# The feed-forward blocks of a two-layer encoder in two sweeps, with the gate and value products in a seven-product form

## The chip, the cores and the metric

One Trainium2 chip, one core. The metric is device microseconds (us) of one execution of the whole program. Several executions of the kernel before were timed, and one was recorded by the hardware profiler; all rows below are of that one.

## What is computed

Two layers over the same 1024 prompt tokens and 64 sample tokens. Each layer is a mixer (layer 0: retention and differential attention; layer 1: band attention and a state-space scan), a product with an output matrix, and a feed-forward block. Only the feed-forward block changes:

```python
x = x + g1 * mixer_out                              # 1024 features
h = rmsnorm(x, norm_g[l, 1]) * (1.0 + sc2) + sh2    # scale and shift from the modulation w_mod[l]
u = h @ w_up[l]                                     # 1024 -> 2 * 2816
a, g = u[..., :2816], u[..., 2816:]
g = causal_dwconv(g, past, conv_w, conv_b)          # width 3, along the tokens
x = x + g2 * ((a * gelu(g)) @ w_down[l])            # 2816 -> 1024
```

All is fp32. A product is emulated by splitting each operand into a high and a low fp32r part and adding three matmuls (high by high, low by high, high by low).

## The kernel before, in words

Activations lie feature-major: 128 features a tile, tokens along the columns, in three chunks c of 386, 386 and 324 columns (two columns of overlap for the convolution, the sample tokens at the end of chunk 2). `x` stays in SBUF for the whole feed-forward block.

The output product (`out_proj`, PSUM tile `ops`) adds into `x` chunk by chunk, and `norm_chunk` follows each chunk: squares on ACT, sums (`nacc`) on POOL and DVE, a transposing matmul `nps`, the reciprocal root on DVE and POOL, a broadcast matmul `nbc`, then `nt` on DVE and the split into `hhi` and `hlo`.

The block itself (`ffn`) goes over 11 pairs j of two 128-column tiles of `w_up`. For each pair it makes the gate tiles (`gps`, six groups of 24 matmuls), the down product of the pair before it (`dps`, 24 groups of 6 matmuls of up to 384 columns, each added into `x` by DVE), and the value tiles (`aps`, six groups of 24). The gated product `yhi`, `ylo` stays in SBUF for one pair; the last two pairs go down together. So a pair is 288 matmuls up and 144 down, and the down product always lies between gate and value products. While chunk 2 is still being normalized, pair 0 works on chunks 0 and 1.

A weight tile (`raw`, 1 MB) is loaded on SP's queue, cast to `whi` on ACT, and its `wlo` is subtracted on POOL, one instruction of 128x2048.

In layer 0 the modulation of layer 1 runs beside the block: 24 units, each two loads `mh`, 16 multiply-adds `macc` of 128x256 on DVE, and a few small matmuls; `side` is called after every group and takes a step at every fourth.

The engines run their instructions in order; the order is set by the scheduler from the written program.

Of the kernel before, what the change touches and what calls it, by code (L numbers as in the profile page):

```python
# [17 lines left out]
P = 128  # L18
# [21 lines left out]
NWA = 10  # L40
NST = 6
# [4 lines left out]
FS = 4  # L46
# [18 lines left out]
NW = 23  # L65
# [43 lines left out]
class PsPools:  # L109
# [7 lines left out]
    def tile(self, tag, name):  # L117
        if tag == "g":
            turn = self.turns[self.n % len(self.turns)]
            self.n += 1  # L120
            if turn:
                return self.shared.tile([P, 512], F32, tag="gs", name=name)
        p, shape = self.t[tag]
        return p.tile(shape, F32, tag=tag, name=name)


def build(ctx, tc, A, O, stop=None):
# [309 lines left out]
    def x_load(xp):  # L437
        x = [xp.tile([P, KT, CN[c]], F32, tag=f"x{c}", name=f"x{c}") for c in range(3)]
        for c in (2, 0, 1):
            for ks in (slice(4, 8), slice(0, 4)):  # L440
# [3 lines left out]
    def resid(x, c, m, ps, gate):  # L444
        for (b, e, s) in SEG[c]:
            stt(x[c][:, m, b:e], ps[:, b:e], gate[:, m, s:s + 1], x[c][:, m, b:e], ALU.mult, ALU.add)

    def out_proj(w, a, x, gate, pp, after, wts):
        def unit(u, c):
            for m in range(2):  # L450
                ps = pp.tile("g", "ops")
                gemm_fm(ps, wts[u], P * m, a[c], CN[c])
                resid(x, c, 2 * u + m, ps, gate)
# [9 lines left out]
    def ffn(l, a, x, gate, pp, w, after, side):  # L463
        ys = {}
        step = [0]

        def tick():
            side(step[0], pp)
            step[0] += 1

        def down(js):
            wds = [load_rows(A["w_down"][l], 256 * j) for j in js]
            for c in range(3):
                n = CN[c]
                for m in range(KT):
                    ps = pp.tile("g", "dps")
                    mms = []
                    for j, (whi, wlo) in zip(js, wds):
                        for k in range(2):
                            yhi, ylo = ys[j, c, k]  # L480
                            wh, wl = whi[:, k, P * m:P * m + P], wlo[:, k, P * m:P * m + P]
                            mms += [(wh, yhi), (wh, ylo), (wl, yhi)]
                    for i, (lt, rh) in enumerate(mms):
                        T.matmul(out=ps[:, 2:n], lhsT=lt, rhs=rh[:, 2:n], start=(i == 0), stop=(i == len(mms) - 1))  # L484
                    resid(x, c, m, ps, gate)
                    tick()
                if js[-1] == NPAIR - 1:
                    after(c)
            for j in js:
                for c in range(3):  # L490
                    for k in range(2):
                        ys.pop((j, c, k))

        ge = {}

        def up_gate(j, wg, c):
            n = CN[c]
            for m in range(2):
                f = 2 * j + m
                ps = pp.tile("g", "gps")  # L500
                gemm_fm(ps, wg, P * m, a[c], n, b=0)
                e = ge[c, m] = w("ge")
                S.activation(out=e[:, :n], in_=ps[:, :n], func=AF.Identity, scale=fcw[l][:, 2, f:f + 1], bias=fcb[l][:, f:f + 1])  # L503
                stt(e[:, 1:n], ps[:, 0:n - 1], fcw[l][:, 1, f:f + 1], e[:, 1:n], ALU.mult, ALU.add)
                stt(e[:, 2:n], ps[:, 0:n - 2], fcw[l][:, 0, f:f + 1], e[:, 2:n], ALU.mult, ALU.add)
                if c == 2:
                    V.tensor_add(e[:, 260:262], e[:, 260:262], fcor[l][:, f, :])
                    tail = ps[:, 256:388].rearrange("p (s x) -> p s x", x=66)[:, :, 0:2]
                    V.tensor_copy(fo[l][:, :, :, f], tail)
                S.activation(out=e[:, :n], in_=e[:, :n], func=AF.Gelu_apprx_tanh)  # L510
                tick()

        def value(j, wa, c):
            n = CN[c]
            for m in range(2):
                ps = pp.tile("g", "aps")
                gemm_fm(ps, wa, P * m, a[c], n)
                e = ge.pop((c, m))
                hi, lo = w("yhi", F32R), w("ylo", F32R)
                V.tensor_mul(e[:, 2:n], ps[:, 2:n], e[:, 2:n])  # L520
                S.copy(hi[:, 2:n], e[:, 2:n])  # L521
                G.tensor_tensor(out=lo[:, 2:n], in0=e[:, 2:n], in1=hi[:, 2:n].bitcast(F32), op=ALU.subtract)  # L522
                ys[j, c, m] = (hi, lo)
                tick()

        for j in range(NPAIR):
            wg = load_cols(A["w_up"][l], DFF + 256 * j, urgent=(j == 0))
            if j == 0:
                wa = load_cols(A["w_up"][l], 256 * j)
                for c in range(3):  # L530
                    up_gate(j, wg, c)
                    value(j, wa, c)
                continue
            for c in range(3):
                up_gate(j, wg, c)
            if j < NPAIR - 1:
                down([j - 1])
            wa = load_cols(A["w_up"][l], 256 * j)
            for c in range(3):
                value(j, wa, c)  # L540
        side(None, pp)
        down([NPAIR - 2, NPAIR - 1])
# [118 lines left out]
    # start: x feature-major, its statistics, and the first modulation feeding the first product  # L661
# [53 lines left out]
    def mod_pe(u, hv):  # L715
# [3 lines left out]
        row = sm.tile([P, 256], F32, tag="mrow", name="mrow", bufs=1)  # L719
# [287 lines left out]
    # differential attention  # L1007
# [339 lines left out]
    def block_tail(l, wout, am, nxt, side, wts):  # L1347
        st = ctx.enter_context(ExitStack())
# [4 lines left out]
        def w(name, dt=F32):  # L1353
            return fp.tile([P, CW], dt, tag="w", name=name, bufs=NW)
        x = x_load(xp)
        acts = {}

        def mid(c):
            if c == 0:
                acts["h"] = new_act()  # L1360
            norm_chunk(c, x, acts["h"], gmod[2 * l + 1], sh_of(l, 1), pp, w)
        out_proj(wout, am, x, gate_of(l, 0), pp, mid, wts)

        def end(c):
            nxt(c, x, pp, w)
        ffn(l, acts["h"], x, gate_of(l, 1), pp, w, end, lambda i, pp: side(i, pp, fp))
# [4 lines left out]
    def to_layer1(c, x, pp, w):  # L1371
        if c == 0:
            acts1["w"] = load_two(wcd, 2560, 2816, True)
            acts1["h"] = new_act()
# [10 lines left out]
    modg = []  # L1385

    def side0(step, pp, fp):
        if not modg:
            modg.append(mod_steps(1, range(24), pp, lambda: fp.tile([P, 512], F32, tag="mh", name="mh", bufs=2)))
        if step is None:  # L1390
            for _ in modg[0]:
                pass
            mod_scale(1, 0)
            mod_scale(1, 1)
        elif step % FS == 0:
# [504 lines left out]
```

## Time and profile before

| | |
|---|---|
| time, median of 3 (lowest, highest) | 3039.9 us (3036.57, 3045.22) |
| span of the profiled execution | 3042.6 us |
| matmul engine (PE) busy | 2917.6 us, 96% of the span |
| VectorE (DVE), ScalarE (ACT), GpSimd (POOL) busy | 1691.7, 983.2, 890.7 us |
| bytes moved | 237.10 MB, mean 78 GB/s |

The page lists busy times, the span in slices and the chain of work that ended last. The time between two starts on the PE is the price of a matmul, since matmuls overlap in its pipeline and the duration shown (0.34 us for 384 columns) is longer than that.

### The profile page before, as it was taken

The numbers are of one execution on the slowest core, as the hardware profiler recorded it, in microseconds if no ns is written. First come the engines' busy times: TensorE is split into PE (matmuls) and PEld (weight loads), VectorE is DVE, ScalarE is ACT, GpSimd is POOL, SyncE is SP. The second block draws the span as 40 slices with busy tenths as digits, with TensorE's granted clock in tenths as the row PEclk, the third lists the DMA queues.
The fourth block names the chain that finished last, engine by engine and source line by source line (L and its number), as shares of the span: only waits on it lengthen the run. The fifth ranks groups of instructions, "written<-read, shape, count | busy, mean of one in ns | idle before, by whom it ended". The sixth has DMA issues, their size and how long they took to land.

```text
span 3042.6 us, 46567 instructions
## 1 busy us (share of the span) xinstructions
PE 2917.6 (96%) x18362; PEld 2827.7 (93%) x18362; DVE 1691.7 (56%) x3897; ACT 983.2 (32%) x2104; POOL 890.7 (29%) x786
## 2 busy tenths in 40 slices
PE   8999999799999999999999999988999999999998
PEld 5999998699999999999989988877999999999997
DVE  6688666737655655655677664454353333433323
ACT  5211355724222222222253335555242222222221
POOL 5332222324322232232242441020252222322231
PEclk9999999999999999999999999999999999999999
DMA  9344321241222222222322331122211111111111
GB/s 295 88 146 135 108 60 51 69 149 63 67 78 79 83 70 70 84 70 72 95 90 62 89 93 54 43 63 89 98 56 42 42 42 42 42 56 42 42 35 60
DMA packets 232704, 237.10 MB, mean 78 GB/s; under 512 B 13571, under 2 KB 217896, under 8 KB 232488
## 3 DMA queue, kind: packets, MB, share of 16 engines
q1 hardware_dynamic: 232487, 234.14, 24.6%
q8 instruction: 145, 2.38, 0.3%
q14 instruction: 72, 0.58, 0.1%
HBM read 197.72 MB, written 36.38 MB: 77 GB/s over the span
## 4 chain that ended last, share of the span: by engine, by line
PE 83%; DVE 8%; ACT 3%; DMA 2%; issue 2%; POOL 1%; SPq 0%; DVEq 0%; POOLq 0%; ACTq 0%
PE dps L484 17%; PE qkps L215 7%; PE aps L201 6%; PE aps L200 6%; PE aps L203 6%; PE gps L200 6%; PE gps L203 6%; PE gps L201 6%; PE ops L215 2%; PE pvps L1771 2%; PE ops L200 1%; PE ops L201 1%; PE ops L203 1%; PE xps L215 1%; PE ptps L1021 1%
## 5 line engine op out<-in xcount | busy, mean ns | idle before, releaser
L183 POOL TENSOR_TENSOR wlo<-raw,whi 128x2048 fp32r<-128x2048 f32 (+2 forms) x100 | 464.1, 4642 | 1108.9 <-ACT whi L182 968.8
L144 DVE SCALAR_TENSOR_TENSOR x<-dps,modT,x 128x384 f32<-128x384 f32 (+2 forms) x640 | 298.1, 494 | 145.0 <-PE dps L484 144.4
L484 PE MATMUL dps<-yhi,whi 128*128 128x384 f32 (+1 forms) x1056 | 350.7, 332 | 6.3 <-DVE sthi L144 4.3
L484 PE MATMUL dps<-ylo,whi 128*128 128x384 f32 (+1 forms) x1056 | 349.0, 331 | 0.0
L484 PE MATMUL dps<-yhi,wlo 128*128 128x384 f32 (+1 forms) x1056 | 348.2, 331 | 0.0
L200 PE MATMUL aps<-hhi,whi 128*128 128x384 f32 (+1 forms) x1056 | 342.7, 329 | 2.8 <-DVE ge L144 2.8
L200 PE MATMUL gps<-hhi,whi 128*128 128x386 f32 (+1 forms) x1056 | 344.0, 330 | 0.0
L201 PE MATMUL gps<-hlo,whi 128*128 128x386 f32 (+1 forms) x1056 | 343.9, 330 | 0.0
L201 PE MATMUL aps<-hlo,whi 128*128 128x384 f32 (+1 forms) x1056 | 342.6, 329 | 0.0
L182 ACT CAST whi<-raw 128x2048 fp32r<-128x2048 f32 (+2 forms) x105 | 191.0, 1825 | 424.8 <-PE dps L484 290.0
L144 DVE SCALAR_TENSOR_TENSOR ge<-gps,pT,ge 128x385 f32<-128x385 f32 (+3 forms) x264 | 156.4, 594 | 298.6 <-ACT ge L503 295.1
L520 DVE TENSOR_TENSOR ge<-aps,ge 128x384 f32<-128x384 f32 x132 | 70.3, 534 | 314.4 <-PE aps L203 314.1
L484 PEld LDWEIGHTS dps<-yhi,whi 128*128 128x128 f32 x1056 | 200.5, 190 | 7.9 <-DVE sthi L144 4.7
L522 POOL TENSOR_TENSOR ylo<-ge,yhi 128x384 fp32r<-128x384 f32 x132 | 130.4, 990 | 249.6 <-ACT yhi L521 219.5
L200 PEld LDWEIGHTS aps<-hhi,whi 128*128 128x128 f32 x1056 | 198.7, 188 | 3.3 <-ACT hhi L316 3.3
L484 PEld LDWEIGHTS dps<-ylo,whi 128*128 128x128 f32 x1056 | 200.4, 190 | 0.1
L484 PEld LDWEIGHTS dps<-yhi,wlo 128*128 128x128 f32 x1056 | 200.0, 190 | 0.1
L200 PEld LDWEIGHTS gps<-hhi,whi 128*128 128x128 f32 x1056 | 198.9, 188 | 0.5
L201 PEld LDWEIGHTS gps<-hlo,whi 128*128 128x128 f32 x1056 | 198.7, 188 | 0.3
L201 PEld LDWEIGHTS aps<-hlo,whi 128*128 128x128 f32 x1056 | 198.7, 188 | 0.0
L203 PE MATMUL gps<-hhi,wlo 128*128 128x386 f32 (+1 forms) x1056 | 198.0, 329 | 0.0
L203 PE MATMUL aps<-hhi,wlo 128*128 128x384 f32 (+1 forms) x1056 | 197.3, 328 | 0.0
(395 smaller groups left out, 6566.5 us busy)
## 6 DMA issues: line engine op xcount, KB each, us to landing
raw<-in_w_up SPq DMA_DIRECT2D x44, 1024.0 KB, 5.2
mh<-in_w_mod SPq DMA_DIRECT2D x96, 256.0 KB, 2.8
raw<-in_w_down SPq DMA_DIRECT2D x22, 1024.0 KB, 5.0
mq<-in_w_mod SPq DMA_DIRECT2D x64, 256.0 KB, 3.3
raw<-in_w_in_ab SPq DMA_DIRECT2D x24, 512.0 KB, 4.4
x<-xspill SPq DMA_DIRECT2D x8, 772.0 KB, 8.5
raw<-in_w_in_cd SPq DMA_DIRECT2D x12, 512.0 KB, 7.2
raw<-in_w_in_cd SPq DMA_DIRECT2D x6, 1024.0 KB, 5.8
```

The costliest lines, as they stand in the source:

```text
L144: V.scalar_tensor_tensor(out=out, in0=in0, scalar=scalar, in1=in1, op0=op0, op1=op1, **kw)
L182: S.copy(hi[:, sl], raw[:, sl])
L183: eng.tensor_tensor(out=lo[:, sl], in0=raw[:, sl], in1=hi[:, sl].bitcast(F32), op=ALU.subtract)
L200: T.matmul(out=ps[:, b:n], lhsT=whi[:, k, mo:mo + P], rhs=ahi[:, k, b:n], start=(first and i == 0), stop=False)
L201: T.matmul(out=ps[:, b:n], lhsT=whi[:, k, mo:mo + P], rhs=alo[:, k, b:n], start=False, stop=False)
L203: T.matmul(out=ps[:, b:n], lhsT=wlo[:, k, mo:mo + P], rhs=ahi[:, k, b:n], start=False, stop=(last and i == len(ks) - 1))
L215: T.matmul(out=ps[:, b:n], lhsT=lt, rhs=rh, start=(i == 0), stop=(i == len(mms) - 1))
L484: T.matmul(out=ps[:, 2:n], lhsT=lt, rhs=rh[:, 2:n], start=(i == 0), stop=(i == len(mms) - 1))
L520: V.tensor_mul(e[:, 2:n], ps[:, 2:n], e[:, 2:n])
L522: G.tensor_tensor(out=lo[:, 2:n], in0=e[:, 2:n], in1=hi[:, 2:n].bitcast(F32), op=ALU.subtract)
L1021: T.transpose(ps[:kk, P * (b - b0):P * (b - b0 + 1)], e[:, P * b:P * b + kk], ident)
L1771: T.matmul(out=ps[:, :P], lhsT=pts[m][:kk, b, :], rhs=vv[:kk, :], start=(b == 0), stop=(b == nb - 1))
```

## The change

The block becomes two sweeps. `Halves` holds x as 16 rows of 128x544 (8 feature tiles by two token halves of 544), loads them by 40 small DMAs, writes x back to HBM after the residual (40 more), and normalizes in place. `ffn_up` goes over 22 tiles f. For each, gate and value weights (two column tiles), the two halves of the 1024 features and the two token halves make a 2x2 block product, which is formed from seven half-size products instead of eight: 168 matmuls of 272 columns where there were 144 of up to 386. The sums that this needs are: once for a layer, of the normalized rows (`first_terms` for products 1 and 2, `last_terms` for 6, 3, 5, 7, 4, all split into high and low parts); for each f, of the weights (`up_terms`: four adds on DVE, seven casts on ACT and seven subtractions on POOL of 128x512); and of the results (five adds of 544 columns from PSUM on DVE). Each f writes its y (high and low, two halves) to HBM in four DMAs of 278 KB.

`ffn_down` then reloads x, and for each pair loads y (two DMAs of 1.1 MB) and 1 MB of `w_down`; its matmuls are those of before (columns 384, 384, 320). The modulation of layer 1 is split: 10 units in layer 0's up sweep (a step at two places of each f), 14 in its down sweep (a step at every third group).

The core of the diff (in `out_proj` only the residual is passed in; `to_layer1` allocates by chunk):

```diff
+        def norm(self, c, gm, sh, pp, w):
...
+            self.spill(c)
+            for k in range(KT):
...
+                    stt(v, v, gm[:, k, s:s + 1], rs[:, r0:r0 + hi - lo], ALU.mult, ALU.mult)
+                    S.activation(out=v, in_=v, func=AF.Identity, bias=sh[:, k, s:s + 1])
...
+        def last_terms(self, w):
...
+            for k in range(4):
+                (x11, x12), (x21, x22) = self.x[k], self.x[4 + k]
+                t1, t3, t2, t4 = (w(f"t{i}") for i in (1, 3, 2, 4))
+                V.tensor_tensor(out=t3, in0=x22, in1=x12, op=ALU.subtract)
+                V.tensor_tensor(out=t2, in0=t3, in1=x11, op=ALU.add)
+                G.tensor_tensor(out=t1, in0=x12, in1=x11, op=ALU.subtract)
+                V.tensor_tensor(out=t4, in0=x21, in1=t2, op=ALU.subtract)
+                for p, src, eng in ((6, t2, V), (3, x22, G), (5, t1, G), (7, t3, V), (4, t4, V)):
...
+                    split(*pair, src, eng)
+                    self.ops[p].append(pair)
+
+    def split(hi, lo, src, eng):
+        S.copy(hi, src)
+        eng.tensor_tensor(out=lo, in0=src, in1=hi.bitcast(F32), op=ALU.subtract)
...
+        for f in range(NF):
+            nxt = up_raw(l, f + 1) if f + 1 < NF else None
+            wt.update(up_terms(raw, False))
...
+            product(1, pa, True, False)
+            S.copy(half(s1f, 2), pa)
+            pb = bank2("pb")
+            product(6, pb, True, False)
+            V.tensor_tensor(out=half(u2f), in0=half(s1f, 2), in1=pb, op=ALU.add)
+            product(2, pa, False, True)
...
+            for i in (1, 2):
+                stt(half(e1f, i), pa, cw[2 - i], half(e1f, i), ALU.mult, ALU.add)
...
+            product(5, pb, False, False)
...
+            product(7, pe_, True, False)
+            V.tensor_tensor(out=half(u4f), in0=half(u4f), in1=pe_, op=ALU.add)
+            product(3, pb, False, True)
...
+            product(4, pe_, False, True)
...
+    def ffn_down(l, x, gate, pp, yp, before, after, side):
...
+        for js in [[j] for j in range(NPAIR - 2)] + [[NPAIR - 2, NPAIR - 1]]:
...
+            parts = [(load_y(j), load_rows(A["w_down"][l], 256 * j)) for j in js]
...
+                out_proj(wout, am, gate_of(l, 0), pp, hv.resid, mid, wts)
+                hv.last_terms(w)
...
+                ffn_up(l, hv, pp, w, lambda: up_.tile([P, 512], F32, tag="s2", name="s2", bufs=1), side)
+                side.end()
...
+        x = x_load(xp)
...
+        ffn_down(l, x, gate_of(l, 1), pp, fp, before, lambda c: nxt(c, x, pp, lambda name, dt=F32: w(name, dt)), side)
```

Three places in the order. First POOL in layer 1, from the end of the output product on. Before, POOL's part of chunk 2's split (`hlo`) stands last, and the weights are far ahead:

```order
L183 TENSOR_TENSOR wlo<-raw,whi 128x2048 [waits DMAHW3_49,Activation_49]
L270 TENSOR_TENSOR nacc<-nacc,nsq 128x324 [waits DMAHW0_49,Activation_49]
L270 TENSOR_TENSOR nacc<-nacc,nsq 128x324 [waits Activation_49,Pool_49] x2
L317 TENSOR_TENSOR hlo_21651<-nt,hhi_21650 128x384 [waits Activation_49] x4
L292 COPY hhi_21652<-hhi_21650 128x8x2
L292 COPY hlo_21653<-hlo_21651 128x8x2 [waits DVE_49,Pool_49]
L282 TENSOR_TENSOR r_22046<-r_22046,mhalf 128x3 [waits DVE_49]
```

After, at the same place; `r` is again the reciprocal root of chunk 2, `t` the sums t1, `row` and `bt` the low parts of terms, and the first `wlo` is that of product 6's weights:

```order
L296 TENSOR_TENSOR r_23327<-r_23327,mhalf 128x3 [waits DVE_49]
L569 TENSOR_TENSOR bt<-row,bt 128x544 [waits Activation_49]
L557 TENSOR_TENSOR t_23387<-row 128x544
L569 TENSOR_TENSOR row<-row 128x544 [waits DMAHW5_49,Activation_49]
L557 TENSOR_TENSOR t_23405<-row 128x544 [waits PE_49]
L569 TENSOR_TENSOR bt<-t_23387,bt 128x544 [waits Activation_49]
L569 TENSOR_TENSOR bt<-t_23405,bt 128x544 [waits Activation_49]
...
L569 TENSOR_TENSOR bt<-t_23451,bt 128x544 [waits Activation_49]
L569 TENSOR_TENSOR wlo<-s_23487,whi 128x512 [waits Activation_49]
L569 TENSOR_TENSOR wlo<-raw,whi 128x512 [waits Activation_49] x2
```

The low part of product 6's weights now stands behind all of the terms of the rows.

Second SP's queue (the DMAs) in layer 1, where the up sweep ends and the down sweep begins. Before, no such place exists; after:

```order
L667 DMA yd_103<-e_28330 128x544 [waits DMAHW1_49,Pool_49]
L678 DMA y<-yd_103 128x2x1088 [waits DMAHW2_49,PE_49]
L678 DMA y<-yd_102 128x2x1088 [waits DMAHW3_49,PE_49]
L678 DMA y<-yd_103 128x2x1088 [waits DMAHW4_49,PE_49]
L678 DMA y<-yd_102 128x2x1088 [waits DMAHW5_49,PE_49]
L678 DMA y<-yd_103 128x2x1088 [waits DMAHW6_49,PE_49]
L678 DMA y<-yd_102 128x2x1088 [waits DMAHW7_49,PE_49]
L183 DMA raw<-in_w_down 128x2x1024 [waits DMAHW0_49,Pool_49]
L455 DMA x_28603<-xspill 128x4x386 [waits DMAHW1_49,PE_49]
L455 DMA x_28603<-xspill 128x4x386 [waits DMAHW2_49]
```

The y of three pairs and a weight tile stand ahead of x.

Third DVE in layer 0's down product. Before, the `macc` of a pair spread over gate, value and down groups; a stretch at the end of one down product:

```order
L144 SCALAR_TENSOR_TENSOR x_7167<-dps,modT_78,x_7167 128x256
L144 SCALAR_TENSOR_TENSOR x_7167<-dps,modT_78,x_7167 128x64
L144 SCALAR_TENSOR_TENSOR macc<-mh,cact,macc 128x256 x6
L520 TENSOR_TENSOR ge<-aps,ge 128x384
L144 SCALAR_TENSOR_TENSOR macc<-mh,cact,macc 128x256 x4
L520 TENSOR_TENSOR ge<-aps,ge 128x384 x3
```

After, they stand between the residual adds of the down sweep alone:

```order
L155 SCALAR_TENSOR_TENSOR x_13488<-dps,modT_78,x_13488 128x384
L155 SCALAR_TENSOR_TENSOR macc<-mh,cact,macc 128x256 x2
L155 SCALAR_TENSOR_TENSOR x_13488<-dps,modT_78,x_13488 128x384
L155 SCALAR_TENSOR_TENSOR macc<-mh,cact,macc 128x256 x2
L155 SCALAR_TENSOR_TENSOR x_13488<-dps,modT_78,x_13488 128x384
L155 SCALAR_TENSOR_TENSOR macc<-mh,cact,macc 128x256
```

About 20 of them now stand among the 24 groups of a pair.

## Rows read from the trace of the kernel before

**Rows 1.** The page: busy time by engine, and the chain by engine.

```profile
PE 2917.6 (96%) x18362; PEld 2827.7 (93%) x18362; DVE 1691.7 (56%) x3897; ACT 983.2 (32%) x2104; POOL 890.7 (29%) x786
...
PE 83%; DVE 8%; ACT 3%; DMA 2%; issue 2%; POOL 1%; SPq 0%; DVEq 0%; POOLq 0%; ACTq 0%
```

**Rows 2.** The chain in time (start, us, what): layer 0, layer 1.

```profile
949.39 6.35 PE dps L484 x36
...
1388.69 3.19 PE dps L484 x18
...
2295.74 24.13 PE dps L484 x144
...
2367.85 24.05 PE dps L484 x144
```

**Rows 3.** PE's timeline (start, us, instruction): 384, 322, 264 and 256 columns.

```profile
2295.76 0.34 PE L484 MATMUL dps<-ylo,whi 128*128 128x384 f32 x1
...
2297.33 0.34 PE L484 MATMUL dps<-ylo,whi 128*128 128x384 f32 x1
...
2312.96 0.31 PE L484 MATMUL dps<-yhi,whi 128*128 128x322 f32 x1
...
2313.86 0.31 PE L484 MATMUL dps<-yhi,whi 128*128 128x322 f32 x1
...
1575.01 0.28 PE L231 MATMUL zps<-whi,hhi 128*128 128x264 f32 x1
...
1578.88 0.29 PE L233 MATMUL zps<-whi,hlo 128*128 128x264 f32 x1
```

**Rows 4.** Stretches after each output product: us, busy PE, PEld, DVE, ACT, POOL.

```profile
725.00:755.00 30.00, 29.07 (x167) 27.94 (x165) 22.47 (x44) 18.41 (x48) 17.89 (x18) 1.00 0.13 43
2219.00:2249.00 30.00, 28.38 (x162) 27.37 (x161) 22.87 (x45) 18.43 (x48) 18.30 (x19) 1.00 0.12 38
```

**Rows 5.** DVE's and POOL's timelines there, layer 0: chunk 1's split, chunk 2's norm.

```profile
732.66 2.40 DVE L144 SCALAR_TENSOR_TENSOR hlo<-nt,modT,hhi 128x384 fp32r<-128x384 f32 x2
...
745.76 4.75 DVE L144 SCALAR_TENSOR_TENSOR nt<-x,gmod,nbc 128x256 f32<-128x256 f32 x16 [4.33 <-PE nbc L287]
...
731.16 3.48 POOL L270 TENSOR_TENSOR nacc<-nacc,nsq 128x324 f32<-128x324 f32 x3
734.61 4.48 POOL L317 TENSOR_TENSOR hlo<-nt,hhi 128x384 fp32r<-128x384 f32 x4
```

**Rows 6.** Groups by shape, DVE, POOL and ACT: mean ns after the comma.

```profile
L144 DVE SCALAR_TENSOR_TENSOR x<-dps,modT,x 128x384 f32<-128x384 f32 x320 | 192.2, 612 | 117.9 <-PE dps L484 117.4
L144 DVE SCALAR_TENSOR_TENSOR macc<-mh,cact,macc 128x256 f32<-128x256 f32 x336 | 181.0, 579 | 9.2 <-DMA mh<-in_w_mod 9.2
L520 DVE TENSOR_TENSOR ge<-aps,ge 128x384 f32<-128x384 f32 x88 | 48.7, 555 | 200.4 <-PE aps L203 200.3
L520 DVE TENSOR_TENSOR ge<-aps,ge 128x322 f32<-128x322 f32 x44 | 21.6, 492 | 114.0 <-PE aps L203 113.8 <-ACT ge L510 0.2
L183 POOL TENSOR_TENSOR wlo<-raw,whi 128x2048 fp32r<-128x2048 f32 x95 | 448.8, 4725 | 1098.5 <-ACT whi L182 958.4 <-DMA x<-xspill 71.9 <-PE ptps L1021 43.2
L522 POOL TENSOR_TENSOR ylo<-ge,yhi 128x384 fp32r<-128x384 f32 x88 | 90.9, 1036 | 178.7 <-ACT yhi L521 178.7
```

**Rows 7.** DVE and POOL around 1170 us: two multiply-adds, one weight tile.

```profile
1170.62 3.98 DVE L144 SCALAR_TENSOR_TENSOR macc<-mh,cact,macc 128x256 f32<-128x256 f32 x1 [0.24 <-DMA mh<-in_w_mod]
...
1174.99 0.47 DVE L144 SCALAR_TENSOR_TENSOR macc<-mh,cact,macc 128x256 f32<-128x256 f32 x1
...
1169.52 4.79 POOL L183 TENSOR_TENSOR wlo<-raw,whi 128x2048 fp32r<-128x2048 f32 x1 [19.06 <-ACT whi L182]
```

**Rows 8.** The stretch in which x and `w_up` are loaded; GB/s last.

```profile
667.00:684.00 17.00, 17.00 (x107) 17.00 (x106) 3.66 (x10) 6.23 (x8) 11.84 (x5) 1.00 1.00 337
```

**Rows 9.** Two stretches of 5 us: PE busy first, granted clock third from last.

```profile
2985.00:2990.00 5.00, 2.85 (x27) 2.58 (x25) 1.77 (x5) 2.61 (x8) 1.70 (x5) 1.00 0.00 0
2990.00:2995.00 5.00, 5.00 (x20) 5.00 (x21) 3.22 (x6) 1.27 (x4) 0.78 (x3) 0.66 0.52 206
```

More of the change, by code (lines that the diff above doesn't have):

```diff
@@ L64 @@
 CLD = 1
-NW = 23
+NW = 8
+NROW = 26
+NU = 8
+ND = 12
 SW = [2.52, 1.701]
@@ L438, in x_load, with out_proj @@
         x = [xp.tile([P, KT, CN[c]], F32, tag=f"x{c}", name=f"x{c}") for c in range(3)]
-        for c in (2, 0, 1):
-            for ks in (slice(4, 8), slice(0, 4)):
+        for c in range(3):
+            for ks in (slice(0, 4), slice(4, 8)):
                 SY.dma_start(out=x[c][:, ks, :CN[c]], in_=xs_d[:, ks, XO[c]:XO[c] + CN[c]])
         return x
[L444 to L448, printed above, removed]
+    def out_proj(w, a, gate, pp, resid, after, wts):
         def unit(u, c):
@@ L483, in down @@
                     for i, (lt, rh) in enumerate(mms):
-                        T.matmul(out=ps[:, 2:n], lhsT=lt, rhs=rh[:, 2:n], start=(i == 0), stop=(i == len(mms) - 1))
-                    resid(x, c, m, ps, gate)
-                    tick()
+                        T.matmul(out=ps[:, :n], lhsT=lt, rhs=rh, start=(i == 0), stop=(i == len(mms) - 1))
+                    for (b, e, s) in SEG[c]:
+                        o = b - (4 if s else 2)
+                        stt(x[c][:, m, b:e], ps[:, o:o + e - b], gate[:, m, s:s + 1], x[c][:, m, b:e], ALU.mult, ALU.add)
@@ L487, in down @@
+                    side.step()
                 if js[-1] == NPAIR - 1:
                     after(c)
[L489 to L540, printed above, removed]
@@ L541, in ffn, with ffn_state @@
-        side(None, pp)
-        down([NPAIR - 2, NPAIR - 1])
+    def ffn_state(l, pp):
         ps = pp.tile("t", "fops")
@@ L1351, in block_tail, with before @@
         pp = PsPools(tc, st, [("g", 4, [P, 512]), ("t", 2, [P, 512])], pgl)
-        def w(name, dt=F32):
-            return fp.tile([P, CW], dt, tag="w", name=name, bufs=NW)
+        w = work(fp, CW, ND)
         x = x_load(xp)
[L1356 to L1366, printed above, removed]
+        ffn_state(l, pp)
+        if l == 0:
+            side.start(range(MU, 24), pp, lambda: fp.tile([P, 512], F32, tag="mh", name="mh", bufs=2), FS)
+        def before():
+            side.end()
+            if l == 0:
+                mod_scale(1, 0)
+                mod_scale(1, 1)
+        ffn_down(l, x, gate_of(l, 1), pp, fp, before, lambda c: nxt(c, x, pp, lambda name, dt=F32: w(name, dt)), side)
         return st
@@ L1383, in to_layer1, with start, step, end @@
         x_spill(x, c)
[L1385 to L1391, printed above, removed]
-                pass
-            mod_scale(1, 0)
-            mod_scale(1, 1)
-        elif step % FS == 0:
-            next(modg[0], None)
-    block_tail(0, A["w_out_ab"][0], am, to_layer1, side0, wts).close()
+    class Modulation:
+        gen, n, every = None, 0, 1
+        def start(self, units, pp, stage, every):
+            self.gen = mod_steps(1, units, pp, stage)
+            self.n, self.every = 0, every
+        def step(self):
+            self.n += 1
+            if self.gen is not None and self.n % self.every == 0:
+                next(self.gen, None)
+        def end(self):
+            for _ in self.gen or ():
+                pass
+            self.gen = None
+    block_tail(0, A["w_out_ab"][0], am, to_layer1, Modulation(), wts).close()
     a = acts1["h"]
```

220 lines of the change are left out of this document (198 added, 22 removed).

## The prediction

> **What bounds the kernel now.** I read the page first, then the chain in order of time, the timelines, the groups by shape and the stretches. PE is busy 96% of the span and carries 83% of the chain [rows 1]. Inside the feed-forward blocks there is nothing else on it: in layer 1 the down block of one pair starts 72.11 us after that of the pair before, and 24.1 of that are its 144 matmuls; in layer 0 six pairs take 439.3 us, 73.2 each [rows 2]. So gate and value tiles cost 48.0 us a pair in layer 1, 24.0 for each f, and 49.1 and 24.55 in layer 0, where the modulation's matmuls lie between. The reader is to see too that PE does not pause between output product and block: 29.1 and 28.4 of the 30 us after it are busy [rows 4], while DVE does chunk 2's `nt` 20.8 us after that stretch begins [rows 5]. Gate and value work on chunks 0 and 1 covers it.
>
> So a saving of matmul time is a saving of span, as long as PE stays fed. The question is what the new order leaves uncovered.
>
> **The products.** Start to start, 384 columns cost 0.174 us (nine steps in 1.57), 322 cost 0.150 (six in 0.90), 264 cost 0.121 (32 in 3.87) [rows 3]. On the line between the last two, 272 columns cost 0.125, and an f costs 168 x 0.125 = 21.0 us for 24.0. If PE were the only bound, 22 x 3.0 = 66 us a layer would be saved, some 130 in all: 2910 us. The seven-product form saves an eighth of the columns, and the shorter matmul gives little of it back.
>
> **The sweep once it runs.** Each product waits for one result of DVE, ACT or POOL that has 3 to 5 us of cover by the order. For each f POOL has seven subtractions of 512 and one of 544. Its price is 0.185 us and 2.22 ns a column, from 2048 columns in 4.725 and 384 in 1.036 [rows 6], so 1.32 and 1.39, together 10.6. DVE has about 18 larger operations. From 0.555 at 384 columns and 0.492 at 322 [rows 6] one of 544 is 0.72, less 0.07 when another follows; five sums and two convolution steps that read PSUM are 7 x 0.65 = 4.6 us; those with both inputs in SBUF (four adds of weights, two steps in two parts each, two multiplications, one split) are 6.1. All fit into 21 us. But [rows 7] show what the latter do beside POOL: a `macc` of two SBUF inputs takes 0.47 alone and 3.98 when POOL's `wlo` began before it, until that ends; DVE's residual adds from PSUM keep 0.61 on the mean of 320 [rows 6]. POOL's 10.6 and DVE's 6.1 so exclude each other for the most part: 16.7 of 21 us in layer 1, and with eight `macc` of some 0.41 20.0 in layer 0. I take 21.5 for an f in layer 1 (21.0 to 22.6) and 22.6 in layer 0 (21.6, which is 21.0 and the modulation's own matmuls, to 24.6).
>
> **The start of the sweep.** This is the largest new cost. Products 1 and 2 need the first token half only; 6, 7, 5, 3, 4 need sums over all tokens, so all of chunk 2's norm, and nothing in the program lies between the output product and them. From the last `ops` matmul on: the queues hold chunk 1's normalization (16 DVE operations, 16 on ACT, some 7 us), then chunk 2's last squares and sums and the root (5 us by my count of the order); `nbc` at 12.5, against 20 before. The 16 in-place steps take 4.75 [rows 5]: 17.5. Then `last_terms`: 24 operations of 544 on DVE, one of weights behind them, and 12 on POOL, every one with SBUF inputs. How the two run side by side is in [rows 5]: DVE's two `hlo` take 1.20 each, POOL's operations beside them 1.16 and 1.12, where POOL alone would take about 0.95 and DVE 0.55. The pair goes at 1.15, not at the longer alone and not quite at the sum. At 544 columns, with 0.2 of it fixed, that is 1.65. Twelve such pairs are 19.8 us, 13 more DVE operations at 0.65 are 8.4, and POOL has begun two operations early (3 us): the terms end 25 us after 17.5, at 43. The casts on ACT keep up, but its copy s1, which product 2 waits for, stands behind all of them, and the low part of product 6's weights stands last in POOL's queue. Five products of 24 matmuls remain, 15 us, and two waits for weights and sums, 4 us: the first f ends at 62 us after the output product, where 21 would be ideal. Bounds: with POOL for nothing beside DVE the terms end at 34, the first f at 53; with the two prices added and no early start, at 51 and 70.
>
> The Trainium skill (SBUF — State Buffer, section Who interferes with whom) says that a DVE instruction with two SBUF inputs and a GpSimd instruction that reads SBUF block each other for the whole instruction. [rows 7] agree (3.98 us behind 4.79); [rows 5] do less than that, 1.15 for a pair of which the parts alone make some 1.5. By the rule a pair would cost 2.04, the terms would end at 48, and each layer would take 5 us more.
>
> In place of 22 x 24.0 + 2 = 530 us, layer 1's up sweep takes 62 + 21 x 21.5 = 513.5: **16.5 less**. Layer 0: 22 x 24.55 + 2 = 542 against 62 + 21 x 22.6 = 536.6: **5.5 less**.
>
> **From up to down.** x was in SBUF before; now it is read again after the y of three pairs and a weight tile, 3 x 2.2 + 1.0 MB, and its first half chunk is 0.8 MB more. The first y load waits for product 5 of the last f, 8.7 us before the sweep ends; the third stands behind product 4. At 337 GB/s [rows 8] 8.4 MB take 25 us; with 2 us, my estimate, for latency and the last y writes the first x is there 27 us after the first issue, 18 after the end of the sweep. PE can do six groups (6 us) without x, since there are six PSUM buffers: **12 us of wait for each layer, 24** (5 to 18 each). After that loads are as much as before and x stays.
>
> **The down sweep.** Its matmuls are those of before. In layer 1 I cost it at nothing: DVE adds 24 times some 0.55, 13 of 24 us, from PSUM, and y of the next pair loads under 24 us. In layer 0 about 20 `macc` stand among the 24 groups of a pair: 13 + 20 x 0.40 + 1 = 22 of 24.1 us, and one `wlo` of 4.7 holds up one of them for most of its length. That makes 26, so 2 us a pair over, some of it taken up by the six buffers: nine pairs, **14 us** (0 to 35).
>
> **The clock.** After the 2.1 us of idle PE in 2985 to 2990 the next stretch ran at a mean of 0.66 granted, so partly at 1.2 and partly at 2.4 GHz: 20 matmuls where some 30 fit [rows 9], 1.7 us lost. Two such places a layer: **7 us**.
>
> At nothing I cost the small DMAs of x (40 loads, at even 1 us each, lie under the output product, which fills the 58 us from the loads in [rows 8] to the start of [rows 4]; if SP were slower, DVE's first residual adds would wait) and the y writes (1.1 MB an f, 52 GB/s, of 337 in [rows 8]).
>
> **Sum.** 3042.6 - 16.5 - 5.5 + 24 + 14 + 7 = 3065.6. The profiled execution is 2.7 us over the median, within the runs' spread of 9; I predict 3065.
>
> **Rivals.** A, *PE stays fed*: the terms overlap (first f at 53, -18 for both layers), an f takes 21.2 and 21.7 (-6, -19), the down sweep's DVE fits (-14), x comes earlier (-8): 3065 - 65 = 3000, **faster** by 40. For it: the steady order has 3 to 5 us of cover everywhere, and in layer 1 DVE is half empty. Against: [rows 7], and that 41 us of wait have no work to fill them. It decides for faster once the terms end before about 34 us and layer 0 keeps 22 us an f.
> B, *DVE and POOL are the bound of the sweep*: every product of layer 0 waits for an operation that waits for POOL, 24.6 an f (+42), 22.0 in layer 1 (+10), the down sweep loses 2 to 3 us a pair more (+10): 3127. It decides from some 23.5 us an f on. For it: 20.0 of 21.6 us exclude each other, in queues that cannot be reordered. Against: before, layer 0's pairs took only 1.5% longer than layer 1's [rows 2].
> C, *the form does not save PE time*: if 272 columns cost as 322, 0.150, an f is 25.2 and the time 3065 + 21 x 3.7 + 21 x 2.6 = 3197. [rows 3] at 264 exclude it but for the change of weights at every matmul, which those rows have too.
>
> **Chances.** Forecast 0.49, A 0.31, B 0.18, C 0.02. A measurement of this kernel tells about 0.3%, 9 us, from no change. The forecast's own bounds reach from 3030 to 3100, so some of it lies within 9 us: faster 0.32, same 0.12, slower 0.56. The range holds A and B: 2990 to 3130.
>
> **What would show it.** In the profile after: PE's rate in the middle of layer 1's sweep (24 matmuls in 3.0 us; 21.0 to 21.5 us from product 1 of one f to the next); a gap of PE after each output product, 25 us long in two or three pieces, its end released by DVE or POOL at a term or at `wlo`; DVE operations of 544 with SBUF inputs at 1.0 us or more there, 0.7 elsewhere; `dps` waiting for PSUM, and so for DVE's first x add and the x load, some 6 us after the sweep's end; in layer 0 `dps` waiting for DVE in each pair. I am wrong if the first gap is under 10 us (then A), or if PE waits in every f of layer 0 (then B).

## The result, and the profile after

The changed kernel takes **3238.1 us** (median of 4 runs, 3232.43 to 3251.76); the kernel before took 3039.32 beside it. The ratio is **1.066** (95% interval 1.0634 to 1.0686). The forecast of 3065 had the sign right and the size wrong, outside its range. The profiled execution has a span of 3230.6 us, and all times below go by that.

The page after, as [rows 1] of before, and then the group of the first weight sum of an f:

```profile
PE 2860.2 (89%) x19418; PEld 2748.9 (85%) x19418; DVE 2158.4 (67%) x4295; ACT 1096.8 (34%) x2394; POOL 1112.1 (34%) x1030
...
PE 17%; DMA 4%; DVE 2%; issue 1%; ACT 0%; POOL 0%; SPq 0%; DVEq 0%; POOLq 0%; ACTq 0%
...
L584 DVE TENSOR_TENSOR raw<-raw 128x512 f32<-128x512 f32 x44 | 45.6, 1037 | 225.9 <-DMA raw<-in_w_up 225.9
```

PE is busy for 57 us less than before, so something was saved; but it stands for 370 us where it stood for 125. The shares of the chain in the second line add up to 24%: the page could not follow it further back, and nothing below rests on it. The third line is the surprise: 44 small sums of weights, which the prediction priced like any other DVE operation, have DVE wait 226 us for a transfer.

PE's starts cut both executions into stretches ("first f" is the time from the last `ops` matmul to the end of the first 168 matmuls of the sweep; the other 21 follow):

| stretch | before | forecast | after | missed by |
|---|---|---|---|---|
| up to layer 0's last `ops` | 725.4 | 725.4 | 739.1 | +14 |
| first f, layer 0 / layer 1 | – | 62 / 62 | 74.1 / 72.6 | +23 |
| each later f, layer 0 | 24.55 | 22.6 | 25.70 | 21 x 3.1 = +65 |
| each later f, layer 1 | 24.0 | 21.5 | 24.02 | 21 x 2.52 = +53 |
| down sweep, layer 0 / layer 1 | 272.5 / 280 | +26 / +12 | 288.7 / 287.4 | -15 |
| last `dps` of layer 0 to first `zps` of layer 1 | 35.2 | 35.2 | 73.6 | +38 |
| layer 1's mixer | 643.9 | 643.9 | 637.6 | -6 |
| clock, on its own | | +7 | (within the above) | -7 |

The right column adds up to 165, which is 3230.6 less 3065.6. Three of its lines carry it: the steady f, the start of the sweep, and the border between the layers. The 14 us ahead of the first block are not one of them: eleven other kernels with the same code up to that point came to 730 to 739, against one of 725 before, and what the difference is stays open.

**The steady f.** PE's timeline in layer 1 (start, us, instruction): one product of 24 matmuls, and 16 us later the first product of the next f, which PE waits for.

```profile
2639.97 0.42 PE L610 MATMUL pe<-bt,whi 128*128 128x272 f32 x2
...
2642.86 0.29 PE L610 MATMUL pe<-row,wlo 128*128 128x272 f32 x1
2642.98 0.29 PE L610 MATMUL pa<-row,whi 128*128 128x272 f32 x1
...
2659.32 0.76 PE L610 MATMUL pa<-row,whi 128*128 128x272 f32 x2 [2.01 <-DVE e L155]
2659.88 0.79 PE L610 MATMUL pb<-bt,whi 128*128 128x272 f32 x2
```

24 matmuls in 3.01 us, 0.125 each: the price of 272 columns was right. At 2659.32 PE has waited 2.01 us for `e`, DVE's convolution step that frees the bank of `pa`. What DVE, POOL and SP's queue did until then:

```profile
2649.08 0.71 DVE L630 TENSOR_TENSOR u<-s,pb 128x544 f32<-128x544 f32 x1
2656.30 1.36 DVE L584 TENSOR_TENSOR raw<-raw 128x512 f32<-128x512 f32 x1 [6.51 <-DMA raw<-in_w_up]
2657.58 1.59 DVE L155 SCALAR_TENSOR_TENSOR e<-pa,pT,e 128x544 f32<-128x544 f32 x2
...
2643.80 4.77 POOL L569 TENSOR_TENSOR wlo<-raw,whi 128x512 fp32r<-128x512 f32 x3 [2.89 <-ACT whi L568]
...
2649.59 0.38 SPq L667 DMA_DIRECT2D yd<-u  x1
2650.07 1.15 SPq L574 DMA_DIRECT2D raw<-in_w_up  x2
```

Read it backwards. The convolution steps (L155) stand in DVE's queue behind a weight sum (L584), and that waits 6.51 us for its tile. The tile's load is issued at 2650.07, because its buffer, one of two, is read by POOL until 2648.57 and a y store stands ahead of the load on SP. This tile is not the next f's but that of the f after it, the 13th load of the sweep while the 11th f is running: in the written program L584 stands behind the next f's convolution steps, and the scheduler has put it a whole f ahead, where its tile is just on its way. DVE does nothing for 6.5 us, not for want of time and not because a load is late for its use, but since its next instruction in order is the wrong one. Over the sweep, DVE's waits (us in total, times, longest), layer 1 and then layer 0, each from its second f on:

```profile
DVE raw L584 <- DMA raw<-in_w_up: 127.1, 19, 7.6
...
DVE raw L584 <- DMA raw<-in_w_up: 80.8, 19, 5.8
```

The rest is the clock. Stretches: us, busy PE, PEld, DVE, ACT, POOL; third from last the granted clock, of which 0.50 is 1.2 GHz and 1.00 is 2.4:

```profile
2635.00:2656.00 21.00, 20.25 (x159) 20.06 (x160) 12.88 (x17) 7.88 (x14) 10.43 (x10) 1.00 0.34 101
2656.00:2662.00 6.00, 3.99 (x22) 3.71 (x21) 5.47 (x7) 2.06 (x4) 4.72 (x4) 0.78 0.03 9
2662.00:2666.00 4.00, 4.00 (x31) 4.00 (x30) 1.32 (x2) 0.78 (x1) 1.52 (x2) 0.90 0.02 4
```

**The start of the sweep**, layer 1 (last `ops` at 2352.9): PE's gap, DVE and POOL from the first sums on, and the stretch in the gap.

```profile
2402.34 0.82 PE L610 MATMUL pa<-bt,whi 128*128 128x272 f32 x2 [28.91 <-ACT s L627]
...
2373.24 0.71 DVE L555 TENSOR_TENSOR t<-row 128x544 f32<-128x544 f32 x1
2373.99 1.74 DVE L556 TENSOR_TENSOR t<-t,row 128x544 f32<-128x544 f32 x1
...
2377.43 1.85 DVE L555 TENSOR_TENSOR t<-row 128x544 f32<-128x544 f32 x1
2379.20 1.85 DVE L569 TENSOR_TENSOR bt<-t,bt 128x544 fp32r<-128x544 f32 x1
...
2375.11 1.81 POOL L557 TENSOR_TENSOR t<-row 128x544 f32<-128x544 f32 x1
2376.89 1.81 POOL L569 TENSOR_TENSOR row<-row 128x544 fp32r<-128x544 f32 x1
...
2380.00:2402.00 22.00, 0.00 (x0) 0.00 (x0) 22.00 (x20) 8.58 (x16) 14.56 (x9) 0.50 0.00 0
```

DVE alone takes 0.71; beside POOL each of the two takes 1.8, one pair at a time. [rows 4] had PE busy for 28 and 29 of 30 us in this place. Now product 1 is done, product 2 waits for s1 behind all the casts, and PE stands 28.91 us with its clock at 1.2 GHz.

**The border.** PE's first instruction after the last output group of layer 0:

```profile
1659.23 0.47 PE L404 MATMUL mps<-ident,macc 128*128 128x128 f32 x1 [16.89 <-DVE macc L155]
```

The last unit of the modulation is not done when the down sweep ends, its transposes stand in PE's order ahead of the norm of layer 1's first chunk, and the norms of all three chunks follow behind it. PE is busy for 41 of the 73.5 us. Before, the norms of the first two chunks lay among the `dps` matmuls; PE there, with the second chunk's sums (`nps`), the last `dps` and layer 1's first product (`acc`):

```profile
1537.36 1.17 PE L278 MATMUL nps<-ones,nacc 128*128 128x1 f32 x10
1538.39 0.40 PE L484 MATMUL dps<-yhi,wlo 128*128 128x322 f32 x1
...
1539.81 0.31 PE L484 MATMUL dps<-yhi,wlo 128*128 128x322 f32 x1
1540.22 0.45 PE L200 MATMUL acc<-hhi,whi 128*128 128x386 f32 x1
```

### The profile page after: what moved, and what is told of

It is laid out like the page before. It is cut to its first block, busy times and chain, and to the rows that moved or that the text cites. A ratio compares the mean times of both kernels' runs of the same rounds, so it can differ in the third digit from the quotient of the medians.

```text
span 3230.6 us, 50910 instructions
## 1 busy us (share of the span) xinstructions
PE 2860.2 (89%) x19418; PEld 2748.9 (85%) x19418; DVE 2158.4 (67%) x4295; ACT 1096.8 (34%) x2394; POOL 1112.1 (34%) x1030
## 5 line engine op out<-in xcount | busy, mean ns | idle before, releaser
L697 PE MATMUL dps<-y,whi 128*128 128x384 f32 (+1 forms) x2112 | 523.0, 332 | 29.4 <-DVE x L155 24.5
L569 POOL TENSOR_TENSOR wlo<-raw,whi 128x512 fp32r<-128x512 f32 x264 | 384.3, 1471 | 391.9 <-ACT whi L568 379.5
L194 POOL TENSOR_TENSOR wlo<-raw,whi 128x2048 fp32r<-128x2048 f32 (+2 forms) x56 | 254.5, 4547 | 667.4 <-ACT whi L193 601.5
L697 PEld LDWEIGHTS dps<-y,whi 128*128 128x128 f32 x2112 | 376.2, 190 | 33.1 <-DVE x L155 27.5
L155 DVE SCALAR_TENSOR_TENSOR x<-dps,modT,x 128x384 f32<-128x384 f32 (+2 forms) x640 | 295.8, 493 | 128.2 <-PE dps L697 110.3
L697 PE MATMUL dps<-y,wlo 128*128 128x384 f32 (+1 forms) x1056 | 347.7, 331 | 0.0
L610 PE MATMUL pb<-bt,whi 128*128 128x272 f32 x1584 | 313.5, 294 | 37.9 <-DVE u L641 34.6
L610 PEld LDWEIGHTS pb<-bt,whi 128*128 128x128 f32 x1584 | 252.4, 192 | 46.1 <-DVE u L641 42.8
L155 DVE SCALAR_TENSOR_TENSOR macc<-mh,cact,macc 128x256 f32<-128x256 f32 x336 | 223.6, 691 | 10.5 <-DMA mh<-in_w_mod 10.4
L610 PE MATMUL pb<-bt,wlo 128*128 128x272 f32 x792 | 230.2, 291 | 0.0
L610 PE MATMUL pe<-row,whi 128*128 128x272 f32 x1056 | 209.5, 289 | 0.0
L584 DVE TENSOR_TENSOR raw<-raw 128x512 f32<-128x512 f32 x44 | 45.6, 1037 | 225.9 <-DMA raw<-in_w_up 225.9
```

What stands on the lines that cost most here:

```text
L155: V.scalar_tensor_tensor(out=out, in0=in0, scalar=scalar, in1=in1, op0=op0, op1=op1, **kw)
L194: eng.tensor_tensor(out=lo[:, sl], in0=raw[:, sl], in1=hi[:, sl].bitcast(F32), op=ALU.subtract)
L569: eng.tensor_tensor(out=lo, in0=src, in1=hi.bitcast(F32), op=ALU.subtract)
L584: V.tensor_tensor(out=a21, in0=a11, in1=a21, op=ALU.subtract)
L610: T.matmul(out=ps[:, t, :], lhsT=lt, rhs=rh, start=(first and i == 0), stop=(i == len(mms) - 1), skip_group_check=not first)
L697: T.matmul(out=ps[:, :n], lhsT=lt, rhs=rh, start=(i == 0), stop=(i == len(mms) - 1))
```

## The experiments

The theory after the result: three waits, each with a place of its own, hold the time, and the seven-product form does save matmul time once they are gone. (1) In the steady f DVE's order lets PE wait for a weight tile's transfer. (2) The first products wait for the sums over all tokens, whose operations on DVE and POOL take turns. (3) The modulation ends too late. The main rivals: DVE and POOL are simply too slow in every f (B of the prediction), or the form saves nothing (C). e1, e3, e5 and e6 ran beside a before of 3049, e7 to e10 beside 3041, e11 to e13 beside 3042. Single runs scatter: layer 1's steady f, with its own code unchanged, came to 24.02, 24.24, 24.40, 24.42, 24.55 and 24.82 in six kernels (the changed one, e7, e5, e12, e9 and e10), which is 17 us over a sweep. Where a run has no interval, I read the stretch that its edit touches.

**e1: the load of weights left out of the steady f.**

```
-        raw = up_raw(l, 0)
+        raws = [up_raw(l, 0), up_raw(l, 1)]
+        raw = raws[0]
-            nxt = up_raw(l, f + 1) if f + 1 < NF else None
+            nxt = raws[(f + 1) % 2] if f + 1 < NF else None
```

> Leaves out the loads of w_up after the first two tiles of each layer: the same two weight tiles are used over and over, so the numbers are not the reference's; all engine work and all other transfers stay. Theory (DVE stands still for the load of w_up, with its reads of PSUM queued behind): the waits of PE inside a running f go, an f takes 21.2 to 21.8 us in layer 1 (24.3 in the changed kernel) and 22 to 23 in layer 0 (26.3), the span is near 3095 us. Rival (DVE and POOL exclude each other on SBUF, and that alone makes the f long): an f stays within 0.7 us of 24.3 and 26.3, the span stays above 3195 us.

Measured: 3137.7 us. An f takes 21.83 in layer 1 (24.02) and 23.67 in layer 0 (25.70), both a little over what was expected. All operations of DVE and POOL are still there, so in layer 1 it was the transfer and not their pace. PE's waits in layer 1's sweep and into the down sweep (us in total, times, longest); the 28.8 is the start:

```profile
PE pa L611 <- ACT s L628: 39.7, 21, 28.8
PE dps L698 <- DVE x L155: 10.5, 1, 10.5
```

**e6: the same load, but DVE's order changed.** The weight sum gets an operand that the convolution steps' result makes, a 1 of 128x1, and so stands behind them. These are the steps of the f just before the one that the weights are for, so the sum also comes a whole f later: the tile that it reads at 2610.90 was on its way from 2583.66 on.

```
+            one = sm.tile([P, 1], F32, tag="one", name="one", bufs=2)
+            V.tensor_scalar(out=one, in0=e1f[:, 543:544], scalar1=0.0, scalar2=1.0, op0=ALU.mult, op1=ALU.add)
-                V.tensor_tensor(out=a21, in0=a11, in1=a21, op=ALU.subtract)
+                stt(a21, a11, one, a21, ALU.mult, ALU.subtract)
```

> All loads stay; the one add of weights that reads the newly loaded tile is held behind the two convolution steps on DVE by a 128x1 operand that depends on them (one more tiny DVE operation per f). Theory (it is the queue behind the waiting add): PE's wait for the convolution steps goes, an f takes 21.3 to 22.3 us in layer 1 and 22.5 to 24 in layer 0, span 3100 to 3130 us. Rival 1 (DVE and POOL exclude each other): no change, above 3195 us. Rival 2 (the load itself is too late for product 1 of the next f): PE waits for the weights in place of the convolution steps, about 3200 us.

Measured: 3163.9 us; layer 1's f 21.98, as good as without the load. DVE's order there now, and that it waits for PE and ACT, not for a transfer:

```profile
2608.26 1.61 DVE L155 SCALAR_TENSOR_TENSOR e<-pa,pT,e 128x544 f32<-128x544 f32 x2 [3.44 <-ACT s L637]
2609.91 0.15 DVE L641 TENSOR_SCALAR one<-e 128x1 f32<-128x1 f32 x1
2610.26 0.72 DVE L646 TENSOR_TENSOR u<-s,pb 128x544 f32<-128x544 f32 x1 [0.20 <-PE pb L613]
2610.90 1.82 DVE L155 SCALAR_TENSOR_TENSOR raw<-raw,one 128x512 f32<-128x512 f32 x1
```

This is the cleanest of the runs: the same transfers, the same arithmetic and one tiny operation more, and 45 us of layer 1 are back. In layer 0 it returned only 0.86 an f, where e1 returned 2.03, and the whole missed its forecast: from the sweep's second f on PE waits there for ACT's copy of `s`, 20.9 us in all, against 7.8 in the changed kernel. Why that copy comes later is not shown.

**e3: the y stores issued from ScalarE's queue**, out of the load's way on SP.

```
-                    SY.dma_start(out=yd[l][i][:, f, HALF * t:HALF * (t + 1)], in_=y.bitcast(F32)[:, :HALF])
+                    S.dma_start(out=yd[l][i][:, f, HALF * t:HALF * (t + 1)], in_=y.bitcast(F32)[:, :HALF])
```

> The stores of y are issued from ScalarE's queue, so that the load of w_up does not stand behind them on SyncE's queue. Theory A (the stores hold the load up): the load is issued up to 1.5 us earlier in each f, about as much less wait for PE plus what the clock loses behind a wait: 22.5 to 23.3 us an f in layer 1, span 3165 to 3195 us. Theory B (the load waits for its buffer, which POOL's last subtraction frees): an f within 0.5 us of 24.3, span 3215 to 3250 us.

Measured: 3160.1 us; 22.76 an f in layer 1, 23.36 in layer 0. It is less clean than e6. The load now goes out 0.03 us after POOL leaves its buffer rather than 1.50, but the scheduler also put one of the two convolution steps ahead of the weight sum:

```profile
2605.91 4.78 POOL L569 TENSOR_TENSOR wlo<-raw,whi 128x512 fp32r<-128x512 f32 x3 [2.91 <-ACT whi L568]
...
2610.72 0.99 SPq L574 DMA_DIRECT2D raw<-in_w_up  x2
...
2615.26 0.79 DVE L155 SCALAR_TENSOR_TENSOR e<-pa,pT,e 128x544 f32<-128x544 f32 x1 [3.36 <-ACT s L634]
2618.78 1.00 DVE L584 TENSOR_TENSOR raw<-raw 128x512 f32<-128x512 f32 x1 [2.74 <-DMA raw<-in_w_up]
2619.70 0.77 DVE L155 SCALAR_TENSOR_TENSOR e<-pa,pT,e 128x544 f32<-128x544 f32 x1
```

**e8: e6 and e3 together.**

> The held-back weight add of e6_order and the stores from ScalarE's queue of e3_yact together. If both act on one and the same wait (the load of w_up), little is left for the second: up sweeps of some 555 us in layer 0 and 528 in layer 1, span 3115 to 3140 us. If they act on different waits, the gains add: span 3080 to 3100 us.

Measured: 3167.4 us, above both forecasts; 21.98 an f in layer 1 and 24.84 in layer 0: what e6 gives alone. In layer 1 both cure the same wait. In layer 0 e6's order takes back part of what e3 had won (23.36): PE waits 21.4 us for ACT's copy of `s` again, where e3 alone has 8.4.

**e10: the sums over all tokens left out**, their five products using product 1's operands (`last_terms` keeps nothing of its loop).

```
+            for p in (5, 6, 7, 3, 4):
+                self.ops[p] = self.ops[1]
```

> Leaves out the sums and splits of the rows for products 6, 5, 7, 3 and 4 (they use the operands of product 1), so those products depend on chunks 0 and 1 only. Theory (DVE's and POOL's 36 operations set the start): from the last ops matmul to product 1 of the second f 36 to 42 us, not 66.7, in both layers; span 3170 to 3180 us. Rival (the load of w_up for the second f holds the first f up in any case): 55 us or more, span above 3205 us.

Measured: 3171.6 us. The first f ends after 43.6 and 43.3 us instead of 74.1 and 72.6: 30 us for each layer are the price of the sums and splits over all tokens and of waiting for them; the work and the wait are not separated here.

**e7: POOL's twelve operations of `last_terms` on DVE.**

```
-                G.tensor_tensor(out=t1, in0=x12, in1=x11, op=ALU.subtract)
+                V.tensor_tensor(out=t1, in0=x12, in1=x11, op=ALU.subtract)
-                for p, src, eng in ((6, t2, V), (3, x22, G), (5, t1, G), (7, t3, V), (4, t4, V)):
+                for p, src, eng in ((6, t2, V), (3, x22, V), (5, t1, V), (7, t3, V), (4, t4, V)):
```

> POOL's 12 operations of the sums of the rows go to DVE, which then has 36. Theory (DVE and POOL take strict turns there, 1.8 us for an operation of either, so POOL adds nothing): DVE alone needs 36 x 0.64 = 23 us and the s1 copy of the first f starts 42 to 47 us after the last ops matmul, not 48.8; span 3220 to 3228 us. Rival (POOL's share runs beside DVE): the start gets later, 52 us or more, span above 3235 us.

Measured: 3227.9 us; the gap ends at 43.9 and 43.4 us after the last `ops` instead of 49.9 and 49.5. One engine alone is faster than two in turns, since DVE now goes at its own price:

```profile
2368.95 0.71 DVE L555 TENSOR_TENSOR t<-row 128x544 f32<-128x544 f32 x1
2369.59 0.72 DVE L569 TENSOR_TENSOR bt<-row,bt 128x544 fp32r<-128x544 f32 x1
2370.22 0.72 DVE L556 TENSOR_TENSOR t<-t,row 128x544 f32<-128x544 f32 x1
2370.86 0.72 DVE L557 TENSOR_TENSOR t<-row 128x544 f32<-128x544 f32 x1
```

**e5: more frequent modulation steps in the down sweep** (`FS = 3` to `FS = 2`).

> One number changes: the modulation takes a step at every second group of layer 0's down sweep, not at every third. Theory (the last units of the modulation end after the down sweep and hold up layer 1's first norm, 38 us between the two kernels): the units end inside the down sweep, the 17 us wait of PE for macc goes, the span falls by 20 to 38 us, to 3193 to 3211 us, with up to 10 us lost in the down sweep. Rival (DVE is full in the down sweep, so what ends earlier there makes the sweep as much longer): within 8 us of 3231.

Measured: 3239.3 us, border 75.7. It tells nothing: on PE the transposes of the modulation stand in the same places as with 3, so the edit did not change what it was meant to change.

**e9: layer 1's modulation left out of the feed-forward blocks.**

```
+    G.memset(modT[1], 0.0)
-                if l == 0:
-                    side.start(range(MU), pp, lambda: w("mh", F32), 1)
-        if l == 0:
-            side.start(range(MU, 24), pp, lambda: fp.tile([P, 512], F32, tag="mh", name="mh", bufs=2), FS)
```

> Leaves out the modulation of layer 1 that runs in layer 0's feed-forward block (set to zero instead, so layer 1 adds nothing to x; all other work stays). Theory (its multiply-adds make layer 0's sweep longer than layer 1's and its late end holds up layer 1's first norm): an f of layer 0 takes 24.3 us as in layer 1, not 26.3 (40 us), the down sweep 10 to 15 us less, and from the last down matmul of layer 0 to the first zps product 36 us, not 74: span near 3140 us. Rival (the order of the norm's own work is what holds up layer 1): that stretch stays above 65 us, span near 3175 us.

Measured: 3163.4 us. The border falls from 73.6 to 41.6; layer 0's f falls from 25.70 to 23.90 and its down sweep from 288.7 to 279.8.

**e12: the modulation kept, but finished earlier**: 16 of its 24 units in the up sweep.

```
-MU = 10
+MU = 16
             product(7, pe_, True, False)
...
+            side.step()
             product(4, pe_, False, True)
```

> Sixteen of the modulation's 24 units in layer 0's up sweep instead of ten (three steps for each f instead of two), so that the last one ends some 300 instructions of PE ahead of the end of the down sweep and the norms of layer 1's first chunks stand beside the last output groups, as in the kernel before. Theory (the border's 38 us are the modulation's late end): border 36 to 45 instead of 73.6; in exchange layer 0's up sweep gets six units more at 3.8 each, +23, and its down sweep -4: 3205 to 3230 in all. Rival (the border is long for another reason, the last residual adds or the weight tile of layer 1): border 65 or more, 3245 to 3260.

Measured: 3229.6 us. Border 41.9, as without modulation; layer 0's up sweep 633.7 for 613.7. The late end was the border's cost, and a unit costs 3.3 us where it was moved to: the border gives back 32 us and the up sweep takes 20, so little is won. Layer 0's last output group and the norm of the first chunk now leave PE only short gaps; the longest between 1655 and 1705:

```profile
1670.78 1.92 PE L292 MATMUL nps<-ones,nacc 128*128 128x1 f32 x10 [2.80 <-DVE nacc L284]
...
1687.31 0.61 PE L212 MATMUL acc<-hlo,whi 128*128 128x324 f32 x1 [4.24 <-DVE hlo L155]
```

**e11: e1, e9 and e10 together.**

> Left out together: the up-projection's loads after f = 1 (the same two weight tiles serve every f), the modulation of layer 1 inside the feed-forward blocks, and the sums and splits of last_terms (products 5, 6, 7, 3, 4 take product 1's operands). Singly these took 100, 75 and 67 us off 3238; their gains in layer 0's up sweep (46, 38 and 35 us of 614) cannot add up fully, since 22 x 21 us of matmuls and some 25 us at the start stay. Theory (these three waits are the whole of what the new form lost): up sweeps 490 to 510 us in layer 0 and 505 to 520 in layer 1, border 42, in all 2975 to 3010, below the kernel before, which means that the seven-product form does save matmul time. Rival (something else in the new sweep holds it, the form itself or the clock): 3050 or more, with an f at 22.5 us or more. The modulation is also missing from the time, some 15 to 20 us of matmul and waits that the kernel before has.

Measured: 2996.7 us; up sweeps 506.6 and 505.2, border 41.3. An f takes 22.09 in layer 0 and 22.04 in layer 1. The gains of the three single runs add up (100, 75 and 67 us, together 242, against 241 here), so the three waits are nearly the whole of the loss, and the form does save PE time, 2 us of 24 an f, not 3. It is no time for the whole computation: the modulation's own work and the 36 operations of sums and splits in each layer are missing too.

**e13: what helps with nothing left out**: e3, e7 and e12.

> What helps without leaving anything out, together: y stores issued from ScalarE's queue, POOL's twelve sums of last_terms on DVE, sixteen modulation units in the up sweep. Singly 3160, 3228 and (expected) about 3220 for 3238; added up 3132. Theory: 3115 to 3150, a ratio of 1.025 to 1.036 to the kernel before, because the three touch different places (steady f, start of the sweep, border). Rival (the modulation's loads collide with the up-projection's again, now that three steps stand in each f): 3155 to 3190. No theory has it below the kernel before: the products that need all tokens still wait some 24 us at each start, and an f still takes 22 us or more.

Measured: 3136.7 us, median of 4 runs, ratio 1.0295 to the kernel before (1.027 to 1.0319). The border is 41.7, the first f 68.0 in both layers, an f 24.16 and 22.94. It gives half of the loss back. No version that computes everything came near the kernel before.

## Why the prediction was right or wrong

- **The matmul of 272 columns, 0.125 us**: right. 24 of them take 3.01 us. Rival C is out.
- **"Each product waits for one result of DVE, ACT or POOL that has 3 to 5 us of cover by the order"**: this step failed, and with 118 us it is most of the error. I counted the operations of DVE and POOL and asked whether they fit into 21 us. They do: DVE is busy 12.88 of 21 us and idle for 6.5 in one piece. What I did not do is read DVE's order as a queue and ask for each instruction in it whether it can itself wait, and for what. L584 waits for a transfer that was issued 6.2 us before; between it and PE stand only the two convolution steps. In layer 1 e6 shows it by order alone, e1 by the transfer alone, which gives back 46 us there and 43 in layer 0. Rival A is out with this step. Rival B came nearer (22.0 and 24.6 an f, where 24.02 and 25.70 were measured), but for another reason; in layer 1 e1 excludes it. In layer 0 two waits of about equal size add up: without the load 2.03 less an f, without the modulation 1.80, without both (and without the sums) 3.61. PE's waits in layer 0 from the second f on, two of the changed kernel and one of e1, whose L662 is L661 here:

```profile
PE pb L610 <- DVE u L641: 31.7, 17, 2.9
PE pe L610 <- DVE u L661: 22.3, 9, 3.2
...
PE pe L611 <- DVE u L662: 20.2, 9, 2.7
```

  L641 stands behind L584 and its wait goes with the load; L661 stands behind the modulation's `macc` and stays. Without the modulation (e9) PE has 39.8 us of waits for the convolution steps instead, as layer 1 has 38.4.
- **The f without waits**: 21.5 was forecast for layer 1; e1, e6 and e11 show 21.8 to 22.0. In e1 PE still waits in nearly each f, for ACT's copy of `s`, about 0.5 us. The term was 0.4 too small; the 21.0 of the matmuls alone was reached nowhere.
- **The start, 62 us**: mis-sized, 74.1 and 72.6. The mechanism and the place are as described. In layer 1 chunk 2's steps end 20.4 us after `ops`, not 17.5; the terms take 28.9 us, not 25, because the pair of operations costs 1.8, not 1.65; so they end at 49.3 instead of 43, and the second product starts at 49.5, behind ACT's copy as forecast. I took [rows 5], where such a pair at 384 columns had gone at 1.15; with 0.2 of that fixed it makes 1.55 at 544 columns, so my 1.65 was also a slip, and without it the forecast would have missed by more. The Trainium skill's rule (SBUF — State Buffer, Who interferes with whom), by which I had the terms end at 48, was nearer; e7 and the rows of turns above agree that the two engines exclude each other, though the pair took less than the rule's 2.04. The remaining 23 us to the end of the first f, where I had 19, are 144 matmuls, 18 us at full clock, some of them at 1.2 GHz.
- **Up to down, 12 us a layer**: right: one gap in each layer.

```profile
1370.24 1.01 PE L697 MATMUL dps<-y,whi 128*128 128x384 f32 x2 [10.09 <-DVE x L155]
...
2946.84 1.01 PE L697 MATMUL dps<-y,whi 128*128 128x384 f32 x2 [10.31 <-DVE x L155]
```

- **Layer 0's down sweep, 14 us from the `macc`**: too much; with the gap taken off the 16 us longer sweep, 6 are left, and e9 gives 9 for the modulation there. Layer 1's extra 7 us are no more than the gap.
- **The border**: missing altogether, 38 us. I saw the modulation in the sweeps and priced its operations, but did not ask when the last unit is done and who stands behind it in PE's order. e9 and e12 show it.
- **The clock, 7 us**: its sign was right; two gaps a layer were counted, while a wait of 2 us in an f also brings one back to 1.2 GHz, which makes the price of each such wait larger than the wait.

## What to carry to other kernels

Price an engine not only by the sum of its operations but by its order: for each instruction that PE waits for, look what stands ahead of it on the same engine, and what that can wait for; a transfer in that place costs PE what the work in hand does not cover of its delay (2.0 of 6.5 us in the rows above) and the clock behind that, and a dummy operand that moves the waiting instruction behind was worth 2 us of 24 in layer 1 (e6). A form that saves a share of the matmuls but needs sums over all tokens before its second product pays for that at the start of each sweep, some 30 us here (e10); the saving must be larger. Work that is spread beside a long loop must be followed to its last piece and to what stands behind that.

## What was not expected of the hardware

DVE and POOL, each with inputs in SBUF only, take turns: one operation of each took 1.8 us together at 544 columns, where DVE alone starts one every 0.64 us (e7) and POOL alone took 1.33 (at 2356.45 in the changed kernel, with DVE idle). Twelve operations moved from POOL to DVE made the start 6 us shorter. A load of two times 512 KB took 6.2 us from issue to the first use. That was no slow transfer: with the y stores beside it all queues moved 299 GB/s from 2650.0 to 2656.3, near the 337 of [rows 8], though the stretch of 21 us shown above has a mean of 101. In the kernel with the stores on another queue it took no less, 8.1 (2610.72 to 2618.78), at 235 GB/s. And a PE wait of 2.01 us was followed by matmuls at the 1.2 GHz price (granted 0.78 and 0.90 in the next two stretches), though PE had been busy at 2.4 GHz for 20 us ahead of it.
